# Gate projections of a hybrid block: stored x for the operand sums, one more Strassen pair, LayerNorm moved into the gates' tiles

## The chip, the cores and the metric

The kernel runs on one core of a Trainium2 chip. The metric is the device time of one execution in microseconds (us). Three runs of the kernel before took 1413.09, 1416.74 and 1418.86 us; their median is 1416.74 us.

The core has a matrix engine (TensorE, PE in the profile, with PEld for its weight loads), VectorE (DVE), ScalarE (ACT), GpSimd (POOL) and a queue that issues DMAs (SyncE, SP). Each engine works through its own queue in order.

## The reference, cut to what matters

One layer over 1024 tokens of width 1024, in float32. Only the first sub-layer matters here:

```python
h = rmsnorm(x, pre_mix_g) * (1.0 + sc1) + sh1          # sc1, sh1: one number a channel
proj = h @ w_in                                        # conv inputs, q k v, and 2 x 1024 gate columns
u = causal_depthwise_conv(u_val * sigmoid(u_gate), conv_w, conv_b)
u = silu(layernorm(u, conv_ln_g, conv_ln_b))           # 512 channels
y_conv = u @ w_conv_out
y_att = stick_breaking_attention(q, k, v) @ w_att_out
merged = sigmoid(g_conv) * y_conv + sigmoid(g_att) * y_att
y = merged @ w_o
```

After it come a residual with an RMSNorm and a SwiGLU feed-forward sub-layer, which the change does not touch.

## The kernel before, in words

**Layout.** Activations lie transposed: channels on the 128 partitions, the 1024 tokens along the free axis, in halves of 512 (CH). The 1024 channels of h are eight tiles, k = 0 to 7. For precision each operand of a matmul is split into a high part in float32r and a low part (the rest), and each product of two operands is three matmuls: high by high, high by low, low by high. The high part is made by ACT (a copy, line 151), the low part by DVE (a subtraction).

**The start (lines 229 to 376).** x is loaded in eight tiles x0 to x7 of pool p0. DVE scales each in place, `x_op` (line 302: x * scale * rstd; this is the modulated x without its shift). ACT then makes hhi[k] (x + shift, line 305), DVE hlo[k] (line 308). hhi and hlo fill all 16 buffers of the pool hp. All of this is traced at a high priority, and DVE and ACT keep the order written.

**Attention and its filler (lines 408 to 608).** Four head pairs run at a high priority (5000 steps ahead). PE has other work in the gaps: convolution, projections, and last the gates that need nothing else.

**The gates.** The 2048 gate columns are 16 tiles of 128, taken as eight pairs (tiles 2i and 2i+1). A pair is a product of a 2 x 2 block matrix of weights (a11, a12 in the weight tile of 2i, a21, a22 in that of 2i+1; the second index is the half of the 1024 input channels) with a 2 x 2 block matrix of h (b11 and b12 are the token halves of the lower channels, b21 and b22 those of the upper ones).
- `NPL = 2` pairs are plain (lines 609 to 615): 2 x 2 banks x 8 channel tiles x 3 = 96 matmuls of 512 columns each.
- Six pairs (`GPAIRS`) go by a Strassen scheme of seven products, each 4 channel tiles x 3 = 12 matmuls. Two of these, a11 by b11 and a12 by b21, need no sums and are done early as filler (lines 616 to 628, `prod0`, line 407, name k in the profile): each in a bank of its own. ACT copies the first to `ee`, which goes to DRAM as e_d0; DVE adds the second to it (line 626), ACT takes the sigmoid.
- The other five products (`other_five`, lines 687 to 712) need sums of weights (s1 to s4, in the four tiles of the tag "s") and sums of h: T1 to T4, for each of the four channel tile pairs j. They use the tag "x" (seven tiles) for the stored first product (ga) and for three results (gv, gw, gc). Their weights come through the three buffers of the tag "wraw" (gw0a, gw0b and so on in the profile).

**T1 to T4 (lines 660 to 670).** For each j, DVE adds hhi and hlo of tiles j and j+4 into two 1024-wide tiles f (lines 662 and 663; two buffers), takes four differences in place (lines 665 to 668), and ACT and DVE split the four sums into T tiles (line 657 on DVE). The pool of f, x, s and T tiles is opened where attention's pools are closed.

**The LayerNorm (`ln_all`, lines 722 to 760).** It reads the convolution's output from DRAM (`cr`, four tiles of 1024), and for each token half: three additions, a matmul with ones for the mean (ACT scales it), four subtractions, four squares on ACT, three additions, a matmul for the variance, rstd (`rstd_from`, lines 142 to 147), four products (line 749). Then for each tile ACT makes a sigmoid and an affine copy, and DVE multiplies them and restores the order of tokens (`csil`, line 758). All its tiles come from hp. It can use the eight buffers of hhi and hlo 0 to 3 once T and the early products have read them. It is traced after the first Strassen pair, with a priority 100 steps earlier than its place (`LN_PRI`). Its split into chi and clo (line 719) follows behind all pairs, and y_conv behind that.

**What sets the order.** Each instruction has a priority, by its place in the program, less an offset in a `high_priority` block. A planner lists the instructions of each engine from these priorities, from when inputs are ready in its own model of time, and from when a tile of the wanted tag is free. Tiles of a tag are reused as their readers finish. A DMA for a tile that isn't free yet stands in its queue with a wait.

Of the kernel before, what the change touches and what calls it, by code (L numbers as in the profile page):

```python
# [10 lines left out]
F32 = mybir.dt.float32  # L11
# [15 lines left out]
PH = 8  # L27
# [11 lines left out]
NPL = 2  # L39
# [5 lines left out]
LN_DVE0 = (0, 1)  # L45
LN_DVE1 = (0, 1)
SILU_POOL = ()
LN_AT = 0
# [25 lines left out]
def tile_block(ctx: ExitStack, tc: tile.TileContext, xT, vecs, ada1, ada2, win, wv, wcv, wat, wo, w1, w2, cvw, out):  # L74
# [17 lines left out]
    e_d0 = [dp.tile([P, CH], F32, name=f"e_d0_{i}") for i in range(KT)]  # L92
    g_d = [dp.tile([P, 2, 2, CH], F32, name=f"g_d{k}") for k in range(FH)]
# [109 lines left out]
    with ExitStack() as s0:  # L203
# [146 lines left out]
        for k in range(KT):  # L350
# [14 lines left out]
            if k:  # L365
                lo_op(k)
            ws = (q0b, k0b, gg0b)
# [42 lines left out]
    with ExitStack() as sC:  # L410
        pc = mkpool(sC, "pc")
        with ExitStack() as sA:
# [203 lines left out]
            for i in GPAIRS:  # L616
                raw = wp.tile([P, T], F32, tag="wraw", name=f"ew{i}")
                load(raw, win[20 + 2 * i])
                e = [sgp.tile([P, CH], F32, tag="sg", name=f"ee{q}_{i}", bufs=2) for q in range(2)]
                k1 = bank(f"k1_{i}")  # L620
                prod0(k1, w_op(f"a11_{i}", raw[:, :CH], act, dve), "B11")
                act.activation(e[0], k1, AF.Copy)
                store(e_d0[i], e[0])
                k2 = bank(f"k2_{i}")
                prod0(k2, w_op(f"a12_{i}", raw[:, CH:], act, dve), "B21")
                dve.tensor_tensor(e[1], k2, e[0], op=ALU.add)
                act.activation(e[1], e[1], AF.Sigmoid, bias=0.0, scale=1.0)
                store(s_d[2 * i][:, :CH], e[1])

    sV.close()  # L630
    with ExitStack() as sG:
# [27 lines left out]

        for j in range(HK):  # L660
            f = [pg.tile([P, T], F32, tag="f", name=f"f{q}_{j}", bufs=2) for q in range(2)]
            dve.tensor_tensor(f[0], hhi[j], hlo[j], op=ALU.add)
# [51 lines left out]
        cacc, chi, clo, yc, wcs = [], [], [], [], {}  # L714
# [7 lines left out]
        def ln_all():  # L722
            for ct in range(CONVT):
                t = hp.tile([P, T], F32, tag="act", name=f"cr{ct}")
                load(t, channels(u_d[ct]))
                cacc.append(t)
            for c in range(NCH):
                cs = slice(c * CH, (c + 1) * CH)
                la, lm, ls = (hp.tile([P, 2, CH], F32, tag="act", name=f"l{nm}{c}") for nm in "ams")
                s0_, s1_, mean = la[:, 0], la[:, 1], lm[:, 0]  # L730
                e0 = dve if c in LN_DVE0 else pool
                e0.tensor_tensor(s0_, cacc[0][:, cs], cacc[1][:, cs], op=ALU.add)
                for ct in (2, 3):
                    e0.tensor_tensor(s0_, s0_, cacc[ct][:, cs], op=ALU.add)
# [3 lines left out]
                for ct in range(CONVT):  # L738
                    dve.tensor_tensor(cacc[ct][:, cs], cacc[ct][:, cs], mean, op=ALU.subtract)
                    if ct == 0:  # L740
                        act.activation(s1_, cacc[ct][:, cs], AF.Square)
# [6 lines left out]
                for ct in range(CONVT):  # L748
                    dve.tensor_tensor(cacc[ct][:, cs], cacc[ct][:, cs], s0_, op=ALU.mult)
# [1039 lines left out]
```

## Time and profile before

| | |
|---|---|
| median of the runs | 1416.74 us (1413.09 to 1418.86) |
| the profiled execution | 1416.97 us |
| its span, first to last instruction | 1415.2 us |
| mean granted TensorE clock | 0.991 |
| HBM read, written | 190.91 MB, 66.58 MB |
| end of attention on PE | 430.2 us |
| early products on PE | 450.0 to 485.6 us |
| last matmul of the gates starts | about 580 us |

A row of a group of instructions names the line, the engine, the operation, output <- inputs, shapes and how many, then the busy time and the mean duration of one, then the engine's idle time just before them and what ended it. In a timeline, a row gives start and length in us, and in brackets the idle time ahead of the instruction and what released it. "x3" in the timeline is that many instructions in a row.

### The profile page before, as it was taken

What the parts mean: (1) busy time and instruction counts of PE and PEld (TensorE: products, weight loads), DVE (VectorE), ACT (ScalarE), POOL (GpSimd) and SP (SyncE); (2) the same over time, 40 slices, a digit from 0 to 9 for tenths busy, and PEclk for the clock granted to TensorE, in tenths of its full rate; (3) what the DMA queues carried; (4) which work ended last, traced back from release to release, by engine and by line L of the source; (5) the groups of instructions that cost most, each with busy time, mean ns of one, the idle gap of its engine ahead of it and who ended that gap; (6) DMA issues with size and microseconds to landing.
All of it is one profiled execution on the core that took longest, in us unless ns stands there. A gap on an engine that the chain in (4) does not pass through costs nothing.

```text
span 1415.2 us, 18817 instructions
## 1 busy us (share of the span) xinstructions
PE 1378.3 (97%) x6822; PEld 1157.6 (82%) x6822; DVE 1059.9 (75%) x1602; ACT 652.7 (46%) x1136; POOL 102.0 (7%) x245
## 2 busy tenths in 40 slices
PE   7999999999999999999999999999999999999996
PEld 4798898998888877787877778888878887888886
DVE  6898687575857788877579878688877776785357
ACT  5375466364554457312356553234434444334441
POOL 0000000000001111000012100001111110000000
PEclk8999999999999999999999999999999999999998
DMA  9212040140453746764935545456777769597833
GB/s 383 74 36 90 16 164 30 46 150 31 122 162 119 260 149 224 281 209 131 345 119 170 182 147 178 157 172 225 247 250 251 259 241 391 172 334 280 281 116 119
DMA packets 91116, 258.72 MB, mean 183 GB/s; under 512 B 9744, under 2 KB 20112, under 8 KB 90000
## 3 DMA queue, kind: packets, MB, share of 16 engines
q1 hardware_dynamic: 75088, 202.99, 42.4%
q0 software_dynamic: 15936, 54.54, 10.4%
q8 instruction: 53, 0.87, 0.2%
q14 instruction: 39, 0.32, 0.1%
HBM read 190.91 MB, written 66.58 MB: 182 GB/s over the span
## 4 chain that ended last, share of the span: by engine, by line
PE 76%; DVE 8%; DMA 6%; issue 5%; ACT 3%; POOL 1%; SPq 0%; DVEq 0%; POOLq 0%; ACTq 0%
PE ka L956 12%; PE ka L1498 8%; PE kc L956 7%; PE pwo L879 6%; PE pb L1498 4%; PE pgv L172 3%; PE pg L172 3%; PE pv L476 3%; PE pcv L456 3%; PE tr L569 2%; PE pgg L172 2%; PE pk L172 2%; PE pq L172 2%; PE k L407 2%; PE pa L1498 2%
## 5 line engine op out<-in xcount | busy, mean ns | idle before, releaser
L548 ACT ACTIVATE ka<-z 128x128 f32<-128x128 f32 (+2 forms) x96 | 47.0, 496 | 54.1 <-PE z L547 49.6
L573 DVE TENSOR_TENSOR alo<-tr,ahi 128x512 fp32r<-128x512 f32 x80 | 53.4, 685 | 21.4 <-ACT ahi L572 20.7
L554 DVE TENSOR_TENSOR_SCAN ka<-ka,eye 128x128 f32<-128x128 f32 (+1 forms) x64 | 52.1, 831 | 21.8 <-ACT ka L548 21.7
L572 ACT ACTIVATE ahi<-tr 128x512 fp32r<-128x512 f32 x80 | 46.7, 603 | 39.1 <-PE av L578 22.9
L1498 PE MATMUL ka<-gt,w2f 128*128 128x512 f32 x264 | 63.5, 390 | 0.2 <-DMA w2f<-w_d 0.2
L559 DVE TENSOR_TENSOR be<-be,ka 128x127 f32<-128x127 f32 (+2 forms) x96 | 51.2, 551 | 11.9 <-ACT be L550 8.5
L1498 PEld LDWEIGHTS ka<-gt,w2f 128*128 128x128 f32 x264 | 49.4, 188 | 11.2 <-issue 1.0
L1064 PE MATMUL ke<-b,w_hi 128*128 128x512 f32 x176 | 55.1, 394 | 0.0
L550 ACT ACTIVATE be<-z 128x127 f32<-128x127 f32 (+2 forms) x96 | 46.5, 497 | 18.4 <-PE tr L569 18.2
L127 DVE SCALAR_TENSOR_TENSOR ada<-ada,cb 128x1024 f32<-128x1024 f32 x32 | 38.8, 1223 | 19.8 <-DMA ada<-in_ada_dram 19.7
L569 PE MATMUL tr<-ident,be 128*128 128x128 f32 x288 | 46.6, 272 | 0.0
L557 DVE TENSOR_TENSOR_SCAN ka<-ka 128x512 f32<-128x512 f32 x32 | 40.4, 1274 | 6.3 <-ACT ka L548 6.3
L578 PE MATMUL av<-ahi,vst 128*128 128x256 f32 x160 | 43.9, 292 | 0.0
L456 PE MATMUL pcv<-ph,cvw 128*128 128x128 f32 x320 | 42.1, 275 | 1.8 <-DMA ph<-v_d 1.8
L579 PE MATMUL av<-alo,vst 128*128 128x256 f32 x160 | 42.2, 290 | 0.0
L456 PEld LDWEIGHTS pcv<-ph,cvw 128*128 128x128 f32 x320 | 39.8, 191 | 2.7 <-issue 1.9
L1064 PEld LDWEIGHTS ke<-b,w_hi 128*128 128x128 f32 x176 | 33.0, 188 | 7.8 <-issue 1.0
L476 PE MATMUL pv<-wv_hi,hhi 128*128 128x256 f32 x128 | 36.6, 286 | 2.3 <-DVE qst L500 1.4
L151 ACT ACTIVATE gt<-X 128x512 fp32r<-128x512 f32 x33 | 20.4, 630 | 39.3 <-PE ka L1498 12.3
L879 PE MATMUL pwo<-mhi,wo_hi 128*128 128x512 f32 x88 | 34.7, 395 | 2.0 <-DVE sga L819 2.0
L476 PE MATMUL pv<-wv_lo,hhi 128*128 128x256 f32 x128 | 36.3, 285 | 0.0
L476 PE MATMUL pv<-wv_hi,hlo 128*128 128x256 f32 x128 | 36.3, 284 | 0.0
(531 smaller groups left out, 4113.5 us busy)
## 6 DMA issues: line engine op xcount, KB each, us to landing
w_d<-w2o POOLq DMA_DIRECT2D x44, 512.0 KB, 7.7
w2f<-w_d SPq DMA_DIRECT2D x44, 512.0 KB, 5.0
ada<-in_ada_dram SPq DMA_DIRECT2D x32, 512.0 KB, 5.4
w2r<-in_w_dram SPq DMA_DIRECT2D x44, 256.0 KB, 3.8
w1g<-in_w_dram SPq DMA_DIRECT2D x21, 512.0 KB, 3.7
w1u<-in_w_dram SPq DMA_DIRECT2D x21, 512.0 KB, 5.4
cvw<-in_cvw_dram SPq DMA_DIRECT2D x20, 512.0 KB, 3.7
ada_w<-in_ada_dram SPq DMA_DIRECT2D x8, 1024.0 KB, 12.0
```

Source lines behind the costliest of these rows:

```text
L172: pe.matmul(bank, st[:, cols], mv[k][:, c * CH:(c + 1) * CH], start=(i == 0 and s == 0), stop=(i == n - 1 and s == 2))
L456: pe.matmul(cv[:, gi * TM:(gi + 1) * TM], wts[n][:, at:at + P], ph[:, g, SH - 1 - d:SH - 1 - d + TM], start=(d == 0), stop=(d == SH - 1))
L476: pe.matmul(pv[:, :256], st[k][:, tcols], mv[:, wc], start=(k == 0 and i == 0), stop=(k == KT - 1 and i == 2))
L548: act.activation(kap[:, s_lo:s_hi], z[:, zo:zo + w], AF.Sigmoid, bias=0.0, scale=-0.125)
L554: dve.tensor_tensor_scan(rev, rev, eye[:, CH - w:][:, ::-1], 0.0, op0=ALU.mult, op1=ALU.add)
L559: dve.tensor_tensor(beta[:, :m], beta[:, :m], kap[:, s_lo + 1:s_lo + 1 + m], op=ALU.mult)
L569: pe.transpose(tr[:, o:o + P], src, ident)
L573: dve.tensor_tensor(alo, tr, ahi, op=ALU.subtract)
L879: pe.matmul(bank_, st[:, cols], mv[k][:, cs], start=(k == 0 and q == 0), stop=(k == KT - 1 and q == 2))
L956: pe.matmul(bank_, st[:, cols], t[:, mv], start=(first and j == 0 and s == 0), stop=(j == HK - 1 and s == 2), skip_group_check=not first)
L1064: pe.matmul(kbs[f], wes[f][st][:, cols], t[:, mv], start=(i == 0 and j == 0 and q == 0), stop=(j == HK - 1 and q == 2), skip_group_check=i ...
L1498: pe.matmul(dst, w[st][:, cols], g[mv], start=first and s == 0, stop=last and s == 2, skip_group_check=more)
```

## The change

- At the start, each modulated x tile is also stored to DRAM (xm_d), on POOL's queue, as soon as DVE has made it.
- `NPL` is 1: seven Strassen pairs and one plain pair.
- The two early products of a pair share one bank: the first is copied out by ACT, the second is then added onto it in the bank, and ACT takes the sigmoid from the bank. The order is: first product of a pair, then the second of the pair before.
- T1 to T4 are built from xm_d instead of hhi + hlo: 16 loads of 256 KB on SP's queue. One of the four sums needs no shift, in three the shift (or the difference of two shifts) comes in by a scalar_tensor_tensor. The four j use the tags f, x, s and x.
- `ln_all` is traced ahead of all pairs, with the same offset of 100. Its inputs go into the two f tiles (cr0, cr1) and four x tiles (the halves of cr2 and cr3), its sums into s tiles, its sigmoids into x tiles, its silu into s tiles, in pieces of 256 columns. Only its results chi and clo use hp, and they are made inside it.

```diff
-NPL = 2
+NPL = 1
...
             if k:
                 lo_op(k)
+            store(xm_d[k], xs[k])
...
+            kes = {}
+
+            def early(i, q):
+                if q == 0:
+                    raw = wp.tile([P, T], F32, tag="wraw", name=f"ew{i}")
+                    load(raw, win[20 + 2 * i])
+                    kes[i] = bank(f"k_{i}"), raw
+                k, raw = kes[i]
+                w = w_op(f"a1{q + 1}_{i}", raw[:, q * CH:(q + 1) * CH], act, dve)
+                prod0(k, w, ("B11", "B21")[q], q == 0)
+                e = sgp.tile([P, CH], F32, tag="sg", name=f"ee{q}_{i}", bufs=2)
+                act.activation(e, k, (AF.Copy, AF.Sigmoid)[q])
+                store(s_d[2 * i][:, :CH] if q else e_d0[i], e)
+
+            for n, i in enumerate(GPAIRS):
+                early(i, 0)
+                if n:
+                    early(GPAIRS[n - 1], 1)
+            early(GPAIRS[-1], 1)
...
+        dsh1 = small.tile([P, HK], F32, name="dsh1")
+        dve.tensor_tensor(dsh1, mod[:, HK:KT], mod[:, 0:HK], op=ALU.subtract)
         for j in range(HK):
-            f = [pg.tile([P, T], F32, tag="f", name=f"f{q}_{j}", bufs=2) for q in range(2)]
-            dve.tensor_tensor(f[0], hhi[j], hlo[j], op=ALU.add)
-            dve.tensor_tensor(f[1], hhi[HK + j], hlo[HK + j], op=ALU.add)
-            b11, b12, b21, b22 = f[0][:, :CH], f[0][:, CH:], f[1][:, :CH], f[1][:, CH:]
+            if j == 0:
+                f = [pg.tile([P, T], F32, tag="f", name=f"f{q}_{j}", bufs=2) for q in range(2)]
+                b11, b12, b21, b22 = f[0][:, :CH], f[0][:, CH:], f[1][:, :CH], f[1][:, CH:]
+            else:
+                b12, b11, b22, b21 = ((xt, st, xt)[j - 1](f"f{q}_{j}") for q in range(4))
+            for b, k, c in ((b12, j, 1), (b11, j, 0), (b22, HK + j, 1), (b21, HK + j, 0)):
+                load(b, xm_d[k][:, c * CH:(c + 1) * CH])
+            sh, ds = mod[:, HK + j:HK + j + 1], dsh1[:, j:j + 1]
             dve.tensor_tensor(b11, b12, b11, op=ALU.subtract)
-            dve.tensor_tensor(b12, b22, b12, op=ALU.subtract)
-            dve.tensor_tensor(b22, b22, b11, op=ALU.subtract)
-            dve.tensor_tensor(b21, b21, b22, op=ALU.subtract)
-            for b, src in (("T2", b22), ("T3", b12), ("T1", b11), ("T4", b21)):
+            dve.scalar_tensor_tensor(b12, b22, ds, b12, op0=ALU.add, op1=ALU.subtract)
+            dve.scalar_tensor_tensor(b22, b22, sh, b11, op0=ALU.add, op1=ALU.subtract)
+            dve.scalar_tensor_tensor(b21, b21, sh, b22, op0=ALU.add, op1=ALU.subtract)
+            for b, src in (("T2", b22), ("T1", b11), ("T3", b12), ("T4", b21)):
                 B0[b, j] = make_t(f"{b}o_{j}", src, act, dve)
...
             for ct in range(CONVT):
-                t = hp.tile([P, T], F32, tag="act", name=f"cr{ct}")
-                load(t, channels(u_d[ct]))
-                cacc.append(t)
+                src = channels(u_d[ct])
+                if ct < 2:
+                    t = pg.tile([P, T], F32, tag="f", name=f"cr{ct}", bufs=2)
+                    halves = [t[:, :CH], t[:, CH:]]
+                    load(t, src)
+                else:
+                    halves = [xt(f"cr{ct}_{c}") for c in range(NCH)]
+                    for c in range(NCH):
+                        load(halves[c], src[:, c * CH:(c + 1) * CH])
+                cr.append(halves)
...
-                la, lm, ls = (hp.tile([P, 2, CH], F32, tag="act", name=f"l{nm}{c}") for nm in "ams")
+                s0_, s1_, mean, sq = (st(f"l{nm}{c}") for nm in ("a", "b", "m", "s"))
...
+            for ct in (2, 3, 0, 1):
+                g, b_ = vec[:, C_LNG + ct:C_LNG + ct + 1], vec[:, C_LNB + ct:C_LNB + ct + 1]
+                hi, lo = (hp.tile([P, T], F32R, tag="act", name=f"{nm}{ct}") for nm in ("chi", "clo"))
+                rows = []
+                for c in range(NCH):
+                    t, sg = cr[ct][c], xt(f"csig{ct}_{c}")
+                    act.activation(sg, t, AF.Sigmoid, bias=b_, scale=g)
+                    act.activation(t, t, AF.Identity, bias=b_, scale=g)
+                    rows.append([v.rearrange("p (r m) -> p r m", m=TM) for v in (t, sg)])
+                for h_ in range(NCH):
+                    o, ms, cs = st(f"csil{ct}_{h_}"), slice(h_ * TM // 2, (h_ + 1) * TM // 2), hs[h_]
+                    om = o.rearrange("p (m r) -> p r m", r=PH)
+                    for c in range(NCH):
+                        a, sg = rows[c]
+                        dve.tensor_tensor(om[:, c * (PH // 2):(c + 1) * (PH // 2)], a[:, :, ms], sg[:, :, ms],
+                                          op=ALU.mult)
+                    copy_to(act, hi[:, cs], o)
+                    dve.tensor_tensor(lo[:, cs], o, hi[:, cs], op=ALU.subtract)
...
         pair_load(GPAIRS[0])
+        with tc.high_priority(offset=LN_PRI):
+            ln_all()
         for q, i in enumerate(GPAIRS):
             if q + 1 < len(GPAIRS):
                 pair_load(GPAIRS[q + 1])
             other_five(i)
-            if q == LN_AT:
-                with tc.high_priority(offset=LN_PRI):
-                    ln_all()
```

More of the change, by code (lines that the diff above doesn't have):

```diff
@@ L92, in tile_block @@
     e_d0 = [dp.tile([P, CH], F32, name=f"e_d0_{i}") for i in range(KT)]
+    xm_d = [dp.tile([P, T], F32, name=f"xm_d{k}") for k in range(KT)]
     g_d = [dp.tile([P, 2, 2, CH], F32, name=f"g_d{k}") for k in range(FH)]
@@ L615, in tile_block @@
                     store(s_d[n][:, c * CH:(c + 1) * CH], sg)
[L616 to L628, printed above, removed]
+            kes = {}
[15 more added lines that the diff above has]
+            early(GPAIRS[-1], 1)
     sV.close()
@@ L745, in ln_all @@
                 pvv = psg.tile([P, CH], F32, tag="ln", name=f"lnv{c}", bufs=1)
                 pe.matmul(pvv, ones, s1_, start=True, stop=True)
[L747 to L760 removed]
+                rstd_from(s0_, mean, s1_, pvv, 512)
```

46 lines of the change are left out of this document (17 added, 29 removed).

## The prediction

> **What bounds the kernel now.** I read the page first: span, engines, and how much of the span TensorE (PE) leaves free.
>
> ```profile
> span 1415.2 us, 18817 instructions
> ## 1 busy us (share of the span) xinstructions
> PE 1378.3 (97%) x6822; PEld 1157.6 (82%) x6822; DVE 1059.9 (75%) x1602; ACT 652.7 (46%) x1136; POOL 102.0 (7%) x245
> ```
>
> PE is busy for all but 36.9 us of the span. So there are only two ways to gain: give PE less to do, or take away one of its few waits. The profiled execution took 1416.97 us, 1.8 us more than its span, and the median of the runs is 1416.74 us; I work from 1417.0 us and take the 0.2 us between them as nothing.
>
> Next the chain that ended last, for the true price of a matmul, since a busy time counts overlapped matmuls twice (a 128x512 one is listed at 389 ns).
>
> ```profile
> 430.22 19.99 PE pg L172 x88
> 450.21 27.20 PE k L407 x120
> ...
> 567.26 4.42 PE ka L407 x12
> ```
>
> 120 early products' matmuls pass in 27.20 us: 227 ns each, a product of 12 in 2.72 us. Attention's last matmul ends at 430.2; behind it run 88 matmuls of the plain gates, then the early products. The last row is slow: 12 matmuls take 4.42 us where 2.72 are due.
>
> Then the stages of the change, as stretches. Columns: stretch, length, busy us (and instructions) of PE, weight loads, DVE, ACT and POOL, granted clock, DMA share, GB/s.
>
> ```profile
> 20.00:30.00 10.00, 7.33 (x47) 6.84 (x46) 9.61 (x14) 5.16 (x9) 0.00 (x0) 0.71 1.03 424
> 45.00:65.00 20.00, 20.00 (x90) 16.46 (x89) 15.72 (x23) 3.73 (x4) 1.59 (x7) 1.00 0.00 1
> 430.20:450.20 20.00, 20.00 (x90) 16.53 (x89) 15.52 (x22) 6.46 (x13) 1.07 (x2) 1.00 0.39 127
> 450.20:485.70 35.50, 35.50 (x159) 29.38 (x158) 32.49 (x50) 20.21 (x38) 6.99 (x13) 1.00 0.64 219
> 522.00:545.00 23.00, 20.81 (x83) 15.99 (x82) 20.52 (x34) 9.91 (x17) 2.16 (x4) 0.93 0.45 152
> 559.00:573.00 14.00, 11.43 (x43) 8.71 (x42) 13.86 (x14) 10.96 (x12) 1.62 (x3) 0.88 0.81 318
> 580.60:665.00 84.40, 83.57 (x369) 68.88 (x367) 67.86 (x99) 19.29 (x19) 0.54 (x1) 1.00 0.63 215
> ```
>
> PE is full from 430 to 522 and again from 580. It loses time in two stretches only: 83 matmuls fill 18.8 us of 23.0, and 43 fill 9.8 of 14.0. That is 4.2 + 4.2 = 8.4 us, idle time and lowered clock together. In both, DVE is nearly full. What ended the two waits, on PE, ACT and DVE:
>
> ```profile
> 531.95 0.73 PE L407 MATMUL kc<-T1o,s1o 128*128 128x512 f32 x2 [2.13 <-ACT s1o L151]
> ...
> 529.54 0.63 ACT L741 ACTIVATE la<-cr 128x512 f32<-128x512 f32 x1 [0.51 <-DVE cr L739]
> 530.20 1.17 ACT L743 ACTIVATE ls<-cr 128x512 f32<-128x512 f32 x2
> ...
> 525.21 2.49 DVE L749 TENSOR_TENSOR cr<-cr,la 128x512 f32<-128x512 f32 x4
> 527.62 0.69 DVE L694 TENSOR_TENSOR gs<-gs,gw4a 128x512 f32<-128x512 f32 x1
> ...
> 567.26 1.19 PE L407 MATMUL ka<-T3o,s3o 128*128 128x512 f32 x2 [2.32 <-DVE gv L701]
> ...
> 561.99 2.28 DVE L758 TENSOR_TENSOR csil<-cr,csig 128x1024 f32<-128x1024 f32 x1
> ```
>
> The first wait is for s1o, which ACT does behind three squares of the LayerNorm, and these wait for DVE, which had just spent 2.4 us on four products by rstd. The second is for a sum that DVE does behind the LayerNorm's silu product. So both losses come from the LayerNorm being pushed in among the gate pairs. The DVE rows also give its true step: four operations in 527.62 - 525.21 = 2.41 us, 0.60 us each.
>
> **The change, part by part.**
>
> *Seven Strassen pairs for six.* A plain pair is 96 matmuls, a Strassen pair 84: 12 x 227 ns = **2.7 us** less on PE, which is full there. Its DVE and ACT work grows: 14 DVE operations for the five late products (8.4 us at 0.60), but over 60 matmuls (13.6 us), so this alone doesn't bind. More important: 72 matmuls leave the filler that PE has after attention, and come back as late products.
>
> *The LayerNorm ahead of the pairs, in the pairs' tiles.* It has no need of hhi's and hlo's buffers any more, and should be over before most pairs run. Then the two losses above go: **8.4 us**. What would be late next is nothing in the stretch from 580.6, where 369 matmuls fill 83.7 of 84.4 us. Together the most that the change can give is 2.7 + 8.4 = 11.1 us, 1405.9 us.
>
> *The stores at the start: nothing.* Eight stores of x (512 KB) go to POOL's queue as each x is made, the last after 58.4:
>
> ```profile
> 57.15 1.27 DVE L302 SCALAR_TENSOR_TENSOR x<-x,scale,rstd 128x1024 f32<-128x1024 f32 x1
> ...
> 50.73 0.10 POOL L553 MEMSET be<- 128x1 f32 x1 [49.15 <-DVE ada_w L127]
> ...
> w_d<-w2o POOLq DMA_DIRECT2D x44, 512.0 KB, 7.7
> ...
> 66.95 0.57 ACT L497 ACTIVATE qst<-pq 64x512 fp32r<-64x512 f32 x1
> ```
>
> POOL idles for 49 us there, and DMA from 45 to 65 us (share 0.00). A store lands in 7.7 us (w_d), so x7 is let go at about 66.6, and the first tile of attention that may lie there is written at 66.95. Without that cover each us would be a us for the first scores, with the V products to fill PE. The first three stores fall where DMA is full (20 to 30 us): 1.5 MB, 3.7 us at 424 GB/s, on loads of ada weights; the range takes half of it.
>
> *What this costs: the new gap.* The pairs can't start until the T operands stand, and PE's filler is now shorter. Before:
>
> ```profile
> 431.60 1.23 DVE L662 TENSOR_TENSOR f<-hhi,hlo 128x1024 f32<-128x1024 f32 x1
> ...
> 478.09 0.69 DVE L657 TENSOR_TENSOR T4o<-f,T4o 128x512 fp32r<-128x512 f32 x1
> ```
>
> T takes DVE from 431.6 to 478.8, and PE has 88 + 144 = 232 matmuls, 52.6 us, to 482.8. After, PE has 232 - 72 = 160, 36.3 us, to **466.5**. What DVE must do by then, at 0.60: 16 sums and 16 low parts of T (19.2 us; eight additions of 1024 columns are gone), the low parts of 14 early weights of which two are done before 430 (7.2), s1, s2 and one low part of the first pair (1.8): 28.2 us. Their inputs now come by DMA, for which the nearest rows are:
>
> ```profile
> xr<-in_xT_dram SPq DMA_DIRECT2D x16, 256.0 KB, 5.9
> ...
> cr<-u_d SPq DMA_DIRECT2D x4, 512.0 KB, 9.6
> ```
>
> The three sums a step that now add a shift cost what plain ones do: the scalar_tensor_tensor at 57.15 takes 1.27 us for 1024 columns, the addition at 431.60 takes 1.23. The x halves: 5.9 us for 256 KB, so about 437 if the tiles come free where they did, at 431.6. 437 + 28.2 = 465.2: the cover is just enough, with nothing to spare. The loads are 16 x 256 KB, with 2 MB of LayerNorm input pulled ahead: 6 MB in some 36 us, 170 GB/s on top of 127 to 219; that stays under the 424 GB/s of 20 to 30 us, but not by much. They wait on SP's queue for a free tile, and behind them there stand the early weights' and the gates' weight loads.
>
> Whatever of the LayerNorm goes first on DVE comes on top. Its statistics are 17 operations a half (20.4 us), its silu 16 products of 256 columns (at least the 8.7 us of the four of 2.2 us) and eight low parts (4.8): 34 us. So the gap lies between 0 and 34 us less what PE's last 1.3 us cover. It can't be below 0. I take **3 us**, near the lower end: before, these instructions were fed in as their inputs came, one between two of the pairs', and its inputs land last (9.6 us, and two of the four need the f tiles of the first T).
>
> By the row at 567.26 a wait of 2.3 us also lowers the clock and costs another 4.42 - 2.72 = 1.7 us. [...] This trace shows the loss after 2.3 us, and the trace decides: I put the 3 us as 1.3 idle and 1.7 of clock.
>
> *The early products in one bank: nothing.* The second waits until ACT has copied the first, with the next pair's first product (2.72 us) between; six DVE sums go, 3.6 us off the path. ACT has the same count.
>
> Sum: 1417.0 - 2.7 - 8.4 + 3.0 = **1409 us** (1408.9).
>
> **The rivals.**
>
> *Slower: the LayerNorm gets DVE and the tiles first, and PE runs dry.* It is marked 100 steps earlier than its place, and its place is now ahead of all pairs, so by its mark it also stands before the T sums. Its first two inputs use the same two f tiles as the first T, its statistics and silu the four s tiles in which the pairs make s1 to s3. If tiles are given out in that order, the first pair waits for nearly all 34 us of it. Then the first late product starts near 437 + 28.2 + 34 = 499 less the work that fits before 437 and the last few low parts (some 10 us): 489, a gap of 22.5 us, and 1405.9 + 22.5 + 1.7 = **1430 us**. It decides from a gap of 16.5 us (1424.1). For it: DVE is full already from 450 to 485 (32.5 of 35.5 us). Against: before, with the same mark, its operations came between those of the pairs.
>
> *No change: the two losses stay.* The pairs also wait on their weights, in three buffers that are let go late:
>
> ```profile
> 513.67 0.69 DVE L693 TENSOR_TENSOR gs<-gw3b 128x512 f32<-128x512 f32 x1 [2.67 <-DMA gw3b<-in_win_dram]
> ```
>
> If this or the order of the pairs, and not the LayerNorm, is the true cause, only the product is gained: 1417.0 - 2.7 = **1414 us**. For it: the weights' ring is unchanged. Against: the rows ahead of both losses are the LayerNorm's.
>
> **How the numbers follow.** My case, a gap of 0 to 8 us, has a chance of 0.58 and gives 1404 to 1415 us, the slower rival 0.27, no change 0.15. A measurement tells 0.5%, 7.1 us, from no change, so 1409.7 and 1424 are the bounds. My case lies on the first: 0.41 below it and 0.17 above. Faster is thus 0.41, same 0.17 + 0.15 = 0.32, slower 0.27. The range must hold most of the slower rival too: 1404 (the most that can be gained, and 2 us of spread) to 1430, which leaves out 0.03 below and about 0.14 above.
>
> **What would show it.** The right steps: 264 early and plain matmuls instead of 336; no PE wait behind csil or cr operations; the first T2 product within 3 us of the last early one, near 467; silu over by about 540; the end of the gates near 568, where it was 580. The slower rival shows as a PE wait of over 15 us between 466 and 490 while DVE is full of cr and csil operations, with the granted clock low behind it. The prediction fails too if T's sums wait for their loads past 445, or if the start moves by over 2 us.

## The result and the profile after

The changed kernel takes 1457.83 us (median of six runs, 1455.33 to 1462.08), the kernel before 1417.64 us beside it (six runs, 1411.40 to 1423.19): a ratio of 1.0291 with a 95% interval of 1.0259 to 1.0323. It is 40 us slower; forecast was 8 us faster, in a range up to 1430 us.

The page of the profile after, the lines that answer to those of before:

```profile
span 1455.4 us, 18904 instructions
## 1 busy us (share of the span) xinstructions
PE 1384.0 (95%) x6810; PEld 1158.0 (80%) x6810; DVE 1056.3 (73%) x1619; ACT 660.0 (45%) x1154; POOL 107.5 (7%) x254
## 2 busy tenths in 40 slices
PE   7999999999998369999999999999999999999996
```

The 12 matmuls fewer are there (6810 for 6822), and in the row of slices TensorE, full before, has one hole. The same place in stretches of 20 us (columns as above: PE, weight loads, DVE, ACT, POOL, granted clock, DMA share, GB/s):

```profile
430.00:450.00 20.00, 18.87 (x84) 14.98 (x82) 10.04 (x16) 9.46 (x18) 3.20 (x6) 1.00 0.95 337
450.00:470.00 20.00, 14.36 (x48) 10.93 (x49) 18.54 (x30) 10.82 (x20) 3.24 (x6) 0.83 0.88 331
470.00:490.00 20.00, 13.51 (x44) 8.04 (x42) 10.01 (x16) 9.10 (x14) 2.16 (x4) 0.79 0.14 54
490.00:510.00 20.00, 2.07 (x2) 0.50 (x2) 13.98 (x25) 14.51 (x21) 0.00 (x0) 0.50 0.00 0
510.00:530.00 20.00, 8.31 (x24) 5.89 (x24) 15.85 (x29) 11.78 (x20) 0.00 (x0) 0.60 0.38 118
530.00:550.00 20.00, 19.99 (x87) 16.29 (x88) 14.00 (x23) 6.71 (x12) 1.62 (x3) 1.00 0.40 133
```

There are two troubles, and the same view cut at their borders gives their sizes:

```profile
479.40:521.90 42.50, 7.44 (x8) 2.00 (x8) 32.01 (x56) 29.35 (x43) 0.54 (x1) 0.52 0.12 37
436.00:479.40 43.40, 36.58 (x142) 27.94 (x140) 28.64 (x46) 21.42 (x38) 6.83 (x13) 0.92 0.78 290
```

From 436 to 479.4 PE does 142 matmuls in 43.4 us (32.2 us at 227 ns); up to 470 us the DMA share is 0.88 to 0.95. Then up to 521.9 PE has next to nothing. From 530 it is full, and so it stays: the two losses of before are gone. The three largest of PE's waits between 425 and 640 (us in total, how many, the longest):

```profile
PE kc L405 <- ACT s1o L148: 21.7, 1, 21.7
PE lnv L763 <- DVE lb L760: 11.5, 2, 7.6
PE k L405 <- ACT ee L625: 6.8, 4, 4.7
```

The hole is one wait cut up by the LayerNorm's own matmuls: for the first weight operand s1o of pair 0. What stands ahead of it, in the chain of waits (start, length, what):

```profile
461.70 14.03 PE k L405 x48
475.73 0.86 PE lnm L751 x2
...
496.38 2.09 PE lnv L763 x2
...
502.55 1.28 ACT L775
503.85 2.22 ACT csig L775 x3
506.07 2.12 ACT cr L776 x3
...
514.74 2.27 DVE csil L783 x5
...
518.74 0.68 DVE gs L703
...
521.82 0.60 DVE s1o L392
```

This is the whole LayerNorm, from the mean (475.73) to the last silu piece, as one string through PE, DVE and ACT. Only then comes `gs`, the sum s1 of pair 0 (518.74), though its weights, issued at 453.0 us, had landed 5.9 us later. No engine is full in the string: from 479.4 to 521.9 (42.5 us) DVE works 32.0 us and ACT 29.4.

**Where the 40 us come from.** I add up what PE loses against 227 ns a matmul. After: 43.4 - 32.2 = 11.2 us up to 479.4; 42.5 us less 8 matmuls = 40.7 in the hole; and 22 late matmuls from 521.9 to 530.0, at a low clock (0.76) and with a wait of 1.0: 8.1 - 5.0 = 3.1. Together 55.0. Off go the 8.4 us of before and 2.7 us of products: 43.9 us. The traces show 42.1 for the stage, from the first plain products to the last of the attention's output (start of the first group's first, and the last start of the second's; first two rows before, then after):

```profile
L172 PE MATMUL pg<-hhi,wg_lo x64: 387/389/481, 400.4 to 449.8; 128*128 128x512 f32 x64
L172 PE MATMUL pya<-ohi,wa_lo x64: 388/389/389, 621.4 to 663.8; 128*128 128x512 f32 x64
```

```profile
L169 PE MATMUL pg<-hhi,wg_lo x32: 389/389/478, 401.5 to 428.6; 128*128 128x512 f32 x32
L169 PE MATMUL pya<-ohi,wa_lo x64: 389/389/389, 664.7 to 707.0; 128*128 128x512 f32 x64
```

663.8 - 400.4 = 263.4 us, and 707.0 - 401.5 = 305.5. I call this the stage's time below; it leaves out the spread of what lies ahead (the stage starts anywhere from 400 to 408 us in the profiles).

### The profile page after: what moved, and what is told of

The parts are those of the page before. It is cut to its first block, busy times and chain, and to the rows that moved or that the text cites. A ratio compares the mean times of both kernels' runs of the same rounds, so it can differ in the third digit from the quotient of the medians.

```text
span 1455.4 us, 18904 instructions
## 1 busy us (share of the span) xinstructions
PE 1384.0 (95%) x6810; PEld 1158.0 (80%) x6810; DVE 1056.3 (73%) x1619; ACT 660.0 (45%) x1154; POOL 107.5 (7%) x254
## 3 DMA queue, kind: packets, MB, share of 16 engines
q0 software_dynamic: 17168, 58.99, 10.8%
## 4 chain that ended last, share of the span: by engine, by line
PE 79%; issue 7%; DVE 6%; DMA 4%; ACT 3%; POOL 1%; SPq 0%; DVEq 0%; POOLq 0%; ACTq 0%
PE ka L981 14%; PE kc L981 8%; PE ka L1523 7%; PE pwo L904 6%; PE ka L405 4%; PE pb L1523 4%; PE pgv L169 3%; PE pya L169 3%; PE pyc L169 3%; PE pv L474 3%; PE kc L405 2%; PE pgg L169 2%; PE pk L169 2%; PE pq L169 2%; PE pcv L454 2%
## 5 line engine op out<-in xcount | busy, mean ns | idle before, releaser
L405 PE MATMUL k<-hhi,a 128*128 128x512 f32 x112 | 38.6, 418 | 6.8 <-ACT ee L625 6.8
L405 PE MATMUL kc<-T1o,s1o 128*128 128x512 f32 x84 | 22.6, 416 | 21.7 <-ACT s1o L148 21.7
L405 PEld LDWEIGHTS kc<-T1o,s1o 128*128 128x128 f32 x84 | 17.0, 204 | 26.9 <-ACT s1o L148 23.2
```

The source lines that it names most:

```text
L405: pe.matmul(bank_, w[st][:, cols], mvs[mv], start=(first and j == 0 and s == 0), stop=(j == HK - 1 and s == 2), skip_group_check=not first)
```

## The experiments

Eighteen kernels were run; the kernel before ran beside each lot, with medians of 1417 to 1419 us. Ratios are to it.

**What makes the hole: the place, the number of pairs, the sums or the tiles?** The first four take one part each out of the change.

Six pairs (`NPL = 2`, else as after):

> The changed kernel with six Strassen pairs and two plain ones again (NPL = 2), all else as changed. Order theory (the LayerNorm stands ahead of the first pair in the s tiles, and PE has nothing to do until it is through): PE gets back 72 matmuls of filler, 16.3 us, and pays 2.7 us for the plain pair: 1457.8 - 13.6 = about 1444 us, still 26 us over the kernel before. Count theory (the missing filler is the whole cause): about 1417 us, no difference from before. Transfer theory (the loads of stored x and the slow stores of early results hold PE up): about 1455 to 1460 us, since six pairs make nearly the same transfers.

LayerNorm as before (own tiles, behind pair 0), the rest as after:

> The changed kernel with the LayerNorm as before: in the buffers of hhi and hlo, traced behind the first pair; stored x, seven pairs and shared banks stay. Order theory: the gap of 42 us between the last early product and the first late one goes, about 1412 to 1420 us. Transfer theory: the early products still end at about 479 instead of 466 us and the T sums still come by DMA, so a loss of 10 to 15 us stays: about 1425 to 1435 us. Count theory: PE is out of work at 467 to 479 us whatever comes first, about 1430 to 1440 us.

LayerNorm as changed, but called behind pair 0:

```diff
-        with tc.high_priority(offset=LN_PRI):
-            ln_all()
         for q, i in enumerate(GPAIRS):
...
             other_five(i)
+            if q == 0:
+                with tc.high_priority(offset=LN_PRI):
+                    ln_all()
```

> The changed kernel with one line moved: the LayerNorm is traced behind the first pair, as before, but still uses the gates' tiles. Order theory: the first pair gets its s tiles first and PE goes on, but the LayerNorm still holds all four s tiles before the second pair, so a gap of 25 to 40 us appears one pair later, with 13.6 us of PE work in front of it: about 1435 to 1450 us. If it is the place in the program alone that matters and not the shared tiles: about 1412 to 1420 us. Transfer theory: about 1450 us.

Sums from hhi + hlo as before, no xm:

> The changed kernel with T1 to T4 from hhi + hlo again and no stored x; seven pairs, shared banks and the LayerNorm in the gates' tiles stay. Transfer theory: 8 MB of transfers are gone, the early products end near 467 instead of 479 us and the late ones start 13 us or more earlier: about 1440 to 1445 us. Order theory: the gap only moves: DVE has eight additions of 1024 columns more (9.6 us) ahead of the LayerNorm, whose tiles come free later: about 1457 to 1470 us.

| run | median, us (range) | ratio (95%) | stage, us |
|---|---|---|---|
| six pairs | 1448.72 (1444.02-1449.91) | 1.0212 (1.0167-1.0256) | 290.3 |
| LayerNorm of before | 1419.60 (1416.10-1424.48) | 1.0010 (0.9989-1.0032) | 267.9 |
| LayerNorm behind pair 0 | 1463.67 (1462.76-1464.61) | 1.0323 (1.0282-1.0365) | 310.3 |
| no xm | 1464.08 (1460.67-1467.59) | 1.0326 (1.0279-1.0374) | 309.8 |

Only the LayerNorm of before takes the hole away. Its place in the program alone does not: called behind pair 0, the changed LayerNorm leaves that pair's products alone (to 492 us) and opens the same hole behind them, 22.1 us of waiting for pair 1's s2o. Nor do xm or the seventh pair make it. The LayerNorm of before and the run without xm came out as the order theory has it. Six pairs took some 5 us more than its 1444 us, and with the LayerNorm behind pair 0 the time lies outside every range given for it; why that run is 6 us slower than after stays open.

The run with the LayerNorm of before changed place and tiles at once. The next starts from it and moves the call back to the changed place, with the changed priority. So against after it gives back the tiles, and with them the pieces of 1024 columns in which before works; no run changes the pieces alone:

```diff
         pair_load(GPAIRS[0])
+        with tc.high_priority(offset=LN_PRI):
+            ln_all()
...
         for q, i in enumerate(GPAIRS):
...
             other_five(i)
-            if q == LN_AT:
-                with tc.high_priority(offset=LN_PRI):
-                    ln_all()
```

> The kernel after, with the LayerNorm of before (in its own act tiles) but called where the change calls it: ahead of pair 0, with the change's priority. Tile theory: the hole of some 40 us comes from the eight s tiles and the x tiles that LayerNorm takes ahead of pair 0 in the gates' own ring, so with other tiles it does not open even at this place; about 1420 us (1414 to 1428), no PE wait of over 8 us between the last early and the first late product. Place theory: LayerNorm called first with a priority of 100 is run first on DVE whatever its tiles; then the hole of the kernel after is there again and the time is 1445 to 1462 us.

1419.37 us (1416.08 to 1424.78), ratio 1.0007 (0.9990 to 1.0025), stage 266.0. The timeline of DVE in it:

```profile
466.47 0.68 DVE L708 TENSOR_TENSOR gs<-gs,gw0a 128x512 f32<-128x512 f32 x1
467.07 0.69 DVE L710 TENSOR_TENSOR gs<-gw0a,gw0b 128x512 f32<-128x512 f32 x1
467.67 0.69 DVE L665 TENSOR_TENSOR T4o<-f,T4o 128x512 fp32r<-128x512 f32 x1
468.28 0.68 DVE L396 TENSOR_TENSOR s1o<-gs,s1o 128x512 fp32r<-128x512 f32 x1
...
474.52 0.69 DVE L746 TENSOR_TENSOR la<-cr,cr 128x512 f32<-128x512 f32 x1 [1.67 <-DMA cr<-u_d]
```

Called first and with the same mark, the LayerNorm now runs second: s1 to s3 of pair 0 are made among the last T sums, over 50 us earlier than in after, and the LayerNorm's operations fall between the pairs'. So **the shared tiles make the hole**: a tag's buffers are given out in program order, pair 0's s1 stands behind the sixteen s tiles of the LayerNorm in a ring of four, and this takes the planner's freedom to put pair 0 first.

Which tiles? Two runs move half of the s tiles each to the act ring: the eight silu outputs, or the eight sums a, b, m, s.

```diff
-                    o, ms, cs = st(f"csil{ct}_{h_}"), slice(h_ * TM // 2, (h_ + 1) * TM // 2), hs[h_]
+                    o, ms, cs = hp.tile([P, T], F32, tag="act", name=f"csil{ct}_{h_}")[:, :CH], slice(h_ * TM // 2, (h_ + 1) * TM // 2), hs[h_]
```

> The kernel after with one thing moved: the eight silu outputs (csil) come out of the act ring instead of the gates' s ring; a, b, m and s of both halves stay in the s ring ahead of pair 0. Tile theory: pair 0's s1 then waits only until the second half's a, b, m and s leave the ring, at about 495 to 505 us in the profile of after instead of 519; the hole shrinks by 15 to 24 us and the time is 1433 to 1445 us. Place theory: the eight tiles do not matter, 1452 to 1462 us.

```diff
-                s0_, s1_, mean, sq = (st(f"l{nm}{c}") for nm in ("a", "b", "m", "s"))
+                s0_, s1_, mean, sq = (hp.tile([P, T], F32, tag="act", name=f"l{nm}{c}")[:, :CH] for nm in ("a", "b", "m", "s"))
```

> The counterpart of the run with the silu outputs moved: LayerNorm's a, b, m and s come out of the act ring, the eight csil tiles stay in the gates' s ring ahead of pair 0. Tile theory in full: pair 0's s1 still stands behind eight csil tiles in a ring of four, so moving the other eight frees little: the hole ends within 8 us of where it ended in after and the time is 1448 to 1458 us. If it were the a, b, m and s tiles that made most of the hole (the run with csil moved gave 10 of the 38 us), moving them would give the other 28: 1425 to 1433 us.

Silu moved: 1447.89 us, ratio 1.0206 (1.0184 to 1.0229). Sums moved: 1461.57 us, 1.0317 (1.0285 to 1.0349), no gain. The second fits the tile theory, since pair 0 still stands behind the silu (PE waits 21.4 us for s1o), though it lies 4 us above the range given. The first gained less than I expected (10 us, not 15 to 24). The chain of waits and PE's timeline of it (start, length, what; the timeline's brackets hold the wait ahead) show why:

```profile
496.79 0.61 ACT s1o L148
...
522.40 0.61 DVE gv L711
```

```profile
497.44 1.22 PE L405 MATMUL kc<-T1o,s1o 128*128 128x512 f32 x2 [7.66 <-ACT s1o L148]
...
524.22 2.88 PE L405 MATMUL ka<-T3o,s3o 128*128 128x512 f32 x12
```

ACT made s1o 23 us earlier (519.45 in after), as expected, and two products of pair 0 went, then two of pair 1. The third of pair 0 (T3o) needs gv to have emptied its bank, and gv comes at 522.40. gv is an x tile, and the x ring is shared as well (cr2, cr3 and eight csig tiles). That the x ring holds it is the likely cause; no run moves the x tiles alone.

**Why the rest gains nothing.** With the hole gone, seven pairs, xm and the shared bank stand at 1419.4 us where 2.7 us of products are saved. The next three runs build on before's LayerNorm and undo more of the change. (The shared bank comes with the changed order of the early products; no run parts the two.)

Early products in two banks, xm kept:

> LayerNorm of before, early products of before (a bank for each of the two), xm and seven pairs kept. Bank theory: the 7.8 us that PE waits for the ee copies in the run with before's LayerNorm, and some 4 us of reduced clock behind them, come from the shared bank; without it 1407 to 1412 us. Transfer theory: the ee copies wait for their two sg buffers, whose stores are late because the sixteen xm loads fill the DMA engines; two banks put that off by one product only, 1415 to 1421 us.

No xm, shared bank kept:

> LayerNorm of before, operand sums of before (from hhi and hlo, no xm), one bank for two early products and seven pairs kept. Transfer theory: with no xm loads the stores of the ee tiles are on time, PE does not wait for ee (under 1 us), and what is left is before with 2.7 us of products saved, less what DVE lacks at the first late products: 1409 to 1417 us. Bank theory: PE still waits some 8 us for ee, 1417 to 1422 us.

The kernel before with seven pairs and nothing else:

> The kernel before with one plain pair for two and nothing else of the change. Count theory: 12 matmuls of 227 ns fewer, 2.7 us, 1415 to 1417 us. Cover theory: the plain pair that becomes a Strassen pair was the work under which DVE got the operand sums ready; without it PE waits for the first late products by some 5 to 15 us, 1420 to 1430 us.

| seven pairs with | median, us | ratio (95%) | stage | last T4 low part | PE's wait for ee |
|---|---|---|---|---|---|
| xm, shared bank | 1419.60 | 1.0010 (0.9989-1.0032) | 267.9 | 472.2 | 7.8 |
| xm, two banks | 1423.67 | 1.0026 (1.0007-1.0044) | 267.2 | 474.4 | 5.4 |
| no xm, shared bank | 1419.42 | 1.0002 (0.9985-1.0020) | 266.8 | 493.2 | 0 |
| neither | 1424.51 | 1.0045 (1.0028-1.0062) | 272.6 | 492.3 | 2.2 |

The run with two banks lies 3 us above the range of the transfer theory; the one without xm lies in the time range of the bank theory although PE doesn't wait for ee at all. So neither theory had both right.

The seventh pair alone **costs** 5.7 us, as the cover theory has it. In its profile the sums are done only at 492, the early products are over by 470, and PE waits for T operands:

```profile
PE ka L407 <- ACT T2o L151: 3.4, 1, 3.4
...
PE ka L407 <- DVE T2o L657: 1.1, 1, 1.1
PE kc L407 <- DVE T1o L657: 1.1, 1, 1.1
```

xm brings the sums forward by 18 to 21 us, as meant, but then PE waits for `ee` instead, and the two come to the same time. The bank is not the cause of that wait: it is there with two banks and xm, and it is gone without xm. The stores of ee go through POOL's queue, the xm loads through SP's. In the run with own tiles at the start and in the one without xm, the tile view of ee says:

```profile
DMA to landing us min/median/max: 2.3/5.5/7.5
```

```profile
DMA to landing us min/median/max: 2.3/3.0/5.8
```

These two runs differ in the LayerNorm's place as well. The run with the LayerNorm of before differs from the second by xm alone: its median is 5.4 us for 3.0, and the DMA share 0.78 from 430 to 450 us and 0.86 from 450 to 470, for 0.54 and 0.71. So with xm the stores land later. But late stores are not the main cause of the wait. In after the stores land sooner than in the run with six pairs and the shared bank alone (below), and yet PE waits 6.8 us for ee in after and not at all in that run. Their rows, in this order:

```profile
DMA to landing us min/median/max: 2.3/3.6/6.9
```

```profile
DMA to landing us min/median/max: 2.4/4.9/7.0
```

What ACT waited for in after between 425 and 530 us, and the chain that ends PE's longest wait for ee (4.7 us, to 461.70), point elsewhere:

```profile
ACT T2o L148 <- DVE f L677: 5.0, 4, 1.9
ACT T4o L148 <- DVE f L678: 2.4, 2, 1.5
```

```profile
459.84 0.67 DVE f L678
...
460.53 0.02 ACT T4o L148
...
461.07 0.59 ACT ee L625
...
461.70 14.03 PE k L405 x48
```

In ACT's list the copy to ee stands behind the high parts of the T operands, and in this trace it does not pass them: the product that it copies has ended at 457.05 us, and the last store from its buffer, issued at 450.63, has landed by 457.5 (6.9 us at most), yet ACT idles for 1.46 us until DVE's sum for T4o is there (460.53). ee starts as soon as T4o is through, with no idle time of its own ahead of it. DVE is nearly full there (18.54 of 20 us from 450 to 470): with xm all T sums fall between 441 and 468 us, where before they were spread from 432 to 479. Of the four waits in after, three (6.5 of 6.8 us) end with an ee that stood behind other work of ACT in this way; only the first, 0.3 us, ends with an ee that waited for a store. With the LayerNorm of before a store ends 1.2 of the 7.8 us, with own tiles at the start 0.9 of the 7.3. With two banks the two waits end with DVE's addition to ee, which stands among the T sums. So the traces put this wait down mainly to the crowding: xm brings the sums into one stretch of two queues in which ee also stands. A late store has an indirect part: the chain in after begins with one that landed 6.6 us after its issue at 436.96 and held up ACT's next weight part, and DVE behind it. How large that part is stays open, since no run changes the order on ACT alone.

What I had not expected is that the shared bank gains 4 to 5 us by the medians (1423.67 to 1419.60, 1424.51 to 1419.42). The intervals of the second pair of runs lie apart, those of the first overlap; I take the gain as likely, and its path is not shown.

**Room for ee.** Four runs try to remove the wait by more room for ee, on the theory that late stores make it. Four buffers for ee, in the ring `beta` that attention has left; then the plain pair behind the early products too; then six pairs; last, the first products put into the dead half of their raw weights.

```diff
-                e = sgp.tile([P, CH], F32, tag="sg", name=f"ee{q}_{i}", bufs=2)
+                e = pa.tile([P, CH], F32, tag="beta", name=f"ee{q}_{i}", bufs=4)
```

> The kernel of the run with LayerNorm's own tiles at the start, with four buffers instead of two for the ee tiles (in the beta ring that attention has left); xm, seven pairs and the shared bank kept. Transfer theory: PE's 7.3 us of waits for ee go to under 1.5 us, the early products end at about 467 us for 480, and the time falls to 1410 to 1416 us. Cover theory: the operand sums are not ready much before 467 to 475 us, so what PE no longer waits for ee it waits for T2 and s2; 1416 to 1421 us.

> As the run with four ee buffers, and the one plain pair's 96 matmuls (21.8 us) traced behind the early products instead of ahead of them. Cover theory: the sums get 21.8 us more cover and the early products leave the time in which xm is loaded, so the losses between 430 and 490 us go; 1404 to 1411 us. If the loss is not about cover but about DVE's total work in the gates, it only moves into the late products: 1413 to 1420 us.

> As the run with four ee buffers, with six pairs (two plain pairs ahead of the early products, as in the kernel before). Cover theory: the second plain pair hides the xm loads and the sums, at 2.7 us more of products than seven pairs; PE waits under 3 us until the first late product, 1411 to 1416 us, at or below the run with seven pairs. If cover is not short, seven pairs are 2.7 us faster than this.

1452.85, 1424.95 and 1458.14 us (ratios 1.0228, 1.0202 to 1.0254; 1.0045, 1.0030 to 1.0061; 1.0279, 1.0256 to 1.0302): all outside what I expected, and by a mistake of mine. `beta` lies in attention's memory, on which the gates' pool opens, so the tiles for xm come free only as the last ee tiles are stored. In the first of the three the xm loads begin at 466 us (434 in after):

```profile
L103 SPq DMA_DIRECT2D f<-xm_d x16: 319/398/952, 466.4 to 493.3; - x16
```

These runs say nothing on the question, beyond what late sums cost: in the first, PE never waits for ee, and yet it takes 33 us more than with two buffers.

```diff
-                e = sgp.tile([P, CH], F32, tag="sg", name=f"ee{q}_{i}", bufs=2)
+                e = sgp.tile([P, CH], F32, tag="sg", name=f"ee{q}_{i}", bufs=2) if q else raw[:, :CH]
```

> LayerNorm in own tiles at the start, xm, seven pairs and the shared bank kept; the first early product of each pair (ee with q = 0) is put into the half of its raw weights that is no longer needed, so that the sg ring's two buffers hold the second products only. The xm loads start where they did, unlike in the runs with four ee buffers. Transfer theory: PE's 7.3 us of waits for ee and the reduced clock behind them go for the most part, 1411 to 1416 us. Cover theory: what PE no longer waits for ee it waits for the operand sums and pair 0's s1 and s2, 1416 to 1421 us.

1431.98 us, ratio 1.0099 (1.0071 to 1.0127): slower by 12.6 us than with the wait, and outside both ranges. The weights' three buffers are now held until the store has landed, and the weights come late (in the chain a store of ew lands at 462.8 us, and only then the next load of ew starts, which lands at 471.8). A stretch, and the larger of PE's waits from 430 to 482 us:

```profile
450.00:470.00 20.00, 15.87 (x65) 11.56 (x64) 19.86 (x33) 13.59 (x25) 3.23 (x6) 1.00 1.02 401
```

```profile
PE k L409 <- ACT a L152: 3.8, 3, 1.4
PE k L409 <- ACT ew L629: 1.0, 2, 0.7
```

DMA is full (401 GB/s). Among the early products PE still waits 5.5 us, now for weights and ew, where it waited 7.3 for ee. The larger loss lies behind them: gw0b, half of pair 0's weights, is issued at 479.7 us instead of 452.9, and s1o follows on ACT at 486.2 instead of 466.0, and PE's other waits up to 640 us are 10.8 us where they were 3.6. How much of the 12.6 us is the ring and how much the full DMA stays open.

**Six pairs again.** If cover is what seven pairs lack, the parts should gain with two plain pairs. Two runs, the shared bank alone on before, and all parts but the seventh pair, with LayerNorm's own tiles:

> The kernel before with the early products in turn in one bank each and nothing else of the change. With seven pairs the shared bank gained 4 to 5 us (1423.7 to 1419.4 and 1424.5 to 1419.4). If that gain is VectorE's, six adds of 0.7 us fewer that come back only where the sums for the late products are late, it is worth little at six pairs, where PE never waits there: 1415 to 1420 us. If it is PE's own, it comes here too: 1412 to 1415 us.

> LayerNorm in own tiles at the start, xm and the shared bank kept, six pairs and two plain pairs as before, two ee buffers. Cover theory: the second plain pair hides the xm loads, PE does not wait for ee, and the loss that seven pairs have there (some 8 us) is gone at the price of 2.7 us of products: 1411 to 1416 us. If the loss is not one of cover, this is 2.7 us slower than seven pairs: 1420 to 1424 us.

1418.82 us (ratio 1.0007, 0.9990 to 1.0024) and 1418.12 us (1.0009, 0.9987 to 1.0031): no difference from before; the second lies between its two ranges. Yet the stage itself is shorter in both profiles, 258.6 and 257.8 us for 263.4, and in the second PE has no wait for ee or for the T operands. Part of this is a later start: the stage begins at 403.4 us in the second and at 400.4 in before, and it ends only 2.6 us earlier (661.2 for 663.8). For these 2.6 us I looked behind the stage. PE's waits from 640 to 700 us, in before and in the second of the two:

```profile
PE pwo L879 <- DVE sga L819: 2.0, 1, 2.0
```

```profile
PE pwo L892 <- DVE sga L832: 4.2, 1, 4.2
```

The product by w_o starts at 666.2 us in before and at 665.8 in this run. So only 0.4 us are left of the 2.6: VectorE delivers the merged tile no sooner. In both profiles its adaLN dots (products that make conditioning numbers of the channels, one VectorE operation and one load each) wait for their loads, 3.1 us between 620 and 668 in before and 4.0 in this run. The last two runs move six of the sixteen dots behind that point, in the six-pair kernel and in before:

```diff
-            ada2_dots(y_conv(n), 2)
+            ada2_dots(y_conv(n), 2 if n < 2 else 1)
...
-                for col in ((), (32, 33), (34, 35), (36, 37), (38,), (39,), ())[n]:
+                for col in ((), (32, 33, 26), (34, 35, 27), (36, 37, 28), (38, 29), (39, 30), (31,))[n]:
```

> The six-pair run with LayerNorm's own tiles, and six of the sixteen adaLN dots (ada, 1.22 us of VectorE and a load each) moved from the convolution's output stage to the six evictions behind it. In the six-pair run the gates and both outputs take 5.6 us less than in before (257.8 us for 263.4 from the first plain product to the last of pya), yet the time is the same and PE then waits 4.2 us for sga before pwo. Floor theory: VectorE's adaLN dots, which wait for their loads, hold sga back, so that pwo starts at 666 us whatever the gates do; with six fewer ahead of it the wait goes under 1.5 us and the time falls to 1411 to 1415 us. If VectorE is as late without them, or the dots are now late for the next LayerNorm, 1417 to 1421 us.

> The control: the kernel before with the same six dots moved and nothing else. Its wait for sga is 2.0 us. Floor theory: at most those 2.0 us are gained, 1414.5 to 1417 us, less than the six-pair run gains. If moving the dots gains as much here (3 us or more), the gates' own gain has no part in it.

1429.22 us (ratio 1.0072, 1.0052 to 1.0093) and 1429.98 us (1.0085, 1.0065 to 1.0104): both are 11 us slower. The wait for sga did shrink to 1.7 us, but the dots are now late for the next norm. In the six-pair run:

```profile
PE psx L917 <- DVE xsum L1045: 5.6, 1, 5.6
PE pwo L891 <- DVE sga L832: 1.7, 1, 1.7
```

Further on PE waits 6.2 us in that run and 6.6 us in the control for the operand gb of a later product, 1.2 in before. So the test does not settle the question of what holds sga back. The profiles show that the wait behind the stage grows by 2.2 us when the stage ends 2.6 us earlier; the other 3.0 us of the shorter stage are its later start in that one profile, and whether that is spread or a cost of the change is not shown. No version beat the kernel before.

## Why the prediction was wrong, point by point

- **A product of 12 in 2.72 us, 2.7 us saved by the seventh pair.** The count holds (6810 matmuls), the gain does not: alone the seventh pair costs 5.7 us, since the plain pair it replaces was PE's cover for the sums (PE's waits for T operands: 6.0 us, none in before). The prediction saw that 72 matmuls leave the filler and took it as no cost of its own.
- **The two losses of 8.4 us go.** They do: no PE wait from 530 us on. The reason given for them, LayerNorm operations among the gate pairs, is not the whole one: with the shared bank alone, and the LayerNorm among the pairs as before, 655 matmuls pass from 486 to 640 us where 634 did, 4.8 us of work more.
- **The stores at the start: nothing.** Right within 1 us: attention's last matmul ends at 431.2 for 430.2.
- **T ready at 465.2.** Measured 467.8, with the first sum at 440.8 where 437 was put. Right.
- **The early products end at 466.5.** They end at 479.4. PE loses 11.2 us there, 6.8 of them waiting for ee; behind the longest wait the clock is low (0.60 from 460 to 465 us), and 48 matmuls take 14.03 us where 10.9 are due. The term "one bank: nothing" counted ACT's copies and not their place: ee stands behind the T operands in ACT's list, and these wait for DVE, whose sums xm has crowded together. The sum for the loads held (297 to 389 GB/s put, 331 to 337 measured). The bank itself is not the cause: PE waits for ee with two banks as well.
- **The new gap: 3 us. This is the step that failed.** It was taken "near the lower end: before, these instructions were fed in as their inputs came". That freedom came with the LayerNorm's own tiles. The diff took it away: pair 0's s1 stands behind the LayerNorm's tiles in the s ring, and the gap became nearly the whole LayerNorm, 42.5 us instead of 3. The split of the 3 us into idle time and lowered clock was not put to the test.
- **The bound of 34 us was too low as well.** It added up DVE's operations (32.0 us measured in the gap, five of pair 0's among them, so the sum was good), but in a string through three engines the steps of the others count too: squares (0.6 us each), sigmoids (0.81) and table loads (1.28) on ACT, ones matmuls at half the clock (0.50 to 0.52; 2.09 us a pair). And the string starts late: the mean's sum is made at 469.4 us, but its matmul runs only at 475.6, behind the 48 early ones in PE's queue.
- **The slower rival** named the mechanism, the s tiles given out in order, and it is what the runs showed. Its 22.5 us were too few by the same error and by the 10 us it took off for work outside the gap: the first late product came at 520.1 us where it put 489, and of the LayerNorm's 58 DVE operations only three had begun by 469.
- **The rival "no change"** gave 1414 us with the two losses left in. Neither the runs without the hole nor those with six pairs reach that.

## What to carry to other kernels

A tile tag is also an order: in these runs whoever allocated first in the program was served first, and a consumer behind it waited for the tiles ahead (the low part of pair 0's s1 came at 521.8 us, with the LayerNorm in tiles of its own at 468.3). An engine's list is an order too: here a copy of 0.6 us that frees a bank stood behind work that waited for another engine, and PE waited 4.7 us for it. Before letting two stages share a ring, ask who stands behind whom in it, and price a stage that becomes one string by the sum of its steps on all engines, not by its busiest engine (42.5 us here, with 32.0 on DVE). Work that hides nothing visible may be cover: taking away the plain product under which the sums were made cost 5.7 us here, where 2.7 us of matmuls were saved.

## What the runs showed of the hardware

In the hole the granted clock falls to 0.50, and a pair of 128x512 ones matmuls takes 2.09 us (496.38) where it took 0.86 us (475.73) right behind other matmuls. Three pairs of 2.09 us lie in the LayerNorm's string (483.27, 486.70 and 496.38), so by my estimate, 3 x (2.09 - 0.86), the low clock makes it 3.7 us longer. In the early products of after, waits of 0.3, 1.2 and 0.6 us leave the clock at 1.00 (440 to 460 us); behind the wait of 4.7 us it is 0.60 from 460 to 465. After the hole the first 22 matmuls took 8.1 us at a clock of 0.76, 1.0 of them a wait, where 5.0 are due.
